# New SBUF addresses for matmul operands, and one VectorE instruction for four tiles, in a streaming encoder step

## The chip, the core and the metric

The kernel runs on one core of a Trainium2 chip. The metric is the device time of one execution, in microseconds (us). Engines are named as in the profile: PE is TensorE's matmul, PEld its weight load, DVE is VectorE, ACT ScalarE, POOL GpSimd, SP SyncE, which issues the DMAs.

## What is computed

One inference step of a one-layer encoder on 2048 prompt frames and 32 sample frames (T = 2080, D = 1024), all in float32:

```python
# norm -> one projection -> two attention groups -> one output projection
qa, ka, va, qb, kb, vb = split_proj(rmsnorm(h, g_attn), w_in)
oa = diff_attn(qa, ka, va)      # 4 heads: softmax(map 1) - lam * softmax(map 2), chunk-causal over all keys
ob = band_attn(qb, kb, vb)      # 8 heads: each 64-frame chunk sees itself and 8 chunks before
h = h + merge(oa, ob) @ w_out
# squared-ReLU MLP, gated input embedding, final norm
c = rmsnorm(h, g_mlp)
h = h + square(relu(c @ w_up)) @ w_down
h = h + sigmoid(h @ w_ple_gate) * (p @ w_ple_proj)
y = rmsnorm(h, g_final)
```

New keys and values are outputs too. The sample frames attend to a cache of 128 rows as well.

## The kernel before

Every product is made of three matmuls. An operand is split into a high part (rounded to the matmul type) and a low part (what is left), and `mm3` adds high x high, high x low and low x high into one PSUM bank; these are lines L220, L221 and L222 of the profile. The splitting is ACT's (high part, L182) and POOL's or DVE's (low part, L167, L177, L188). In a matmul row such as `vps<-wh,aH` the first name behind the arrow is the moving operand, whose columns stream through the array (256, 272 or 512 here), and the second is the stationary one (128 x 128).

The frames are cut into four blocks: 512, 512, 512 and 544 columns; the last is worked on as two halves of 272 columns. The stages, with the tiles that the change touches:

- Projection (`vwide`, `vtile`, `proj`). Values: `vps`, moving operand the value weights (`wh0`, `wl0` with 512 columns in the first stretch; `wh`, `wl` as two sets of [4, 256] afterwards, made by `wunit`), stationary the activations aH and aL. Queries and keys: `qps`, moving operand the activations.
- Long-range attention (`attn_a_pair`): scores `s` from the keys `ka` (moving), exponent, transposes `tpp` into `pH` and `pL`, and `o`, whose moving operand is `pH` or `pL` with 256 columns. Band attention (`attn_b_pair`) has scores `sb` and the sum `ob` from `pb`. Projections of other blocks are woven between the steps of attention; a list scheduler with its own timeline sets the order on every engine.
- Output projection `ops`, MLP (`ups`, `dps`) and gate (`gps`, `pps`). Blocks 0 and 1 use a plain MLP. Blocks 2 and 3 use `mlp7`, which makes seven quarter products in place of eight: `ups` from the ring `cs` (256 or 272 columns), then `dps` from `uh` and `ul`. These two, the parts of the output projection (`ou`), of the gate (`hu`) and of the input embedding (`pT`), and a few temporaries live in one ring of 20 tiles on the right side of SBUF, the pool `uh`, called up: the late ring. Each of its tiles has 544 columns (2176 bytes). Weights come as halves named `piece`.
- Final norm (`final`). For block 3, its last form (`end`) scales the tiles by the gain beforehand and multiplies at the end by the row factor y, half by half: tile 7 on DVE (L1405), tiles 5 and 6 on POOL (L167), tiles 4 and 3 to 0 on DVE (L1413), with a store after tile 4 and one after tile 0.

Pools take their addresses from two stacks, one from each end of a partition; a small tile opened first, such as `edge`, shifts all that comes after it.

Of the kernel before, what the change touches and what calls it, by code (L numbers as in the profile page):

```python
# [13 lines left out]
F32 = mybir.dt.float32  # L14
F32R = mybir.dt.float32r
# [5 lines left out]
P = 128  # L21
# [121 lines left out]


class Kern:
    def __init__(self, tc, a):
        self.tc = tc
        self.nc = tc.nc
        self.a = a
        self.nt = 3  # L150
        self.pieces = None

    def dma(self, dst, src):
# [455 lines left out]
    def attn_a_pair(self, g, j, ka, ba, pool, ps_s, ps_t, ps_o, late, first=None):  # L609
# [186 lines left out]
    def attn_b_pair(self, h, j, kt, v, kb, bb, q, t1, pool, ps_s, ps_t, ps_o, step, late):  # L796
# [9 lines left out]
        for qi, t in enumerate(tiles):  # L806
# [37 lines left out]
            def second(qi=qi, nr=nr, kts=kts, held=held, end=t is tiles[-1]):  # L844
                if qi == 0:
                    px.append(pool.tile([P, 6, 2, 256], F32R, tag="p", bufs=2, name="pb"))
                p = px[0]
                e = held[0]
# [65 lines left out]
    def oload(self, b, wk, up, out, r=None):  # L914
# [8 lines left out]
        elif up.whole:  # L923
            oact = [up.tile([P, 8, up.aw], F32R, tag="act", name="oact") for _ in range(2)]
            oact = [[t[:, k, :n] for k in range(8)] for t in oact]
        else:
            oact = [[up.tile([P, up.aw], F32R, tag="u", name="ou")[:, :n] for k in range(8)] for _ in range(2)]
        out[b] = oact
# [60 lines left out]
    def cparts(self, b, wk, cs, out, r):  # L989
# [34 lines left out]
    def cstage(self, b, up, out, r):  # L1024
# [6 lines left out]
        def parts(k, *which):  # L1031
            for x, raw in which:
                t = up.tile([P, up.aw], F32R, tag="u", name="cst")[:, :n]
                self.split(t[:, :m], t[:, m:], raw, "act", "dve")
                self.dma(out[x][:, :, k], t.rearrange("p (i c) -> p i c", i=2))

        late = ()
        for k in range(4):
            c = []
            for i in range(2):  # L1040
                tmp = up.tile([P, up.aw], F32, tag="u", name="ct")[:, :n]
                kk = k + 4 * i
# [127 lines left out]
    def mlp7(self, b, hh, box, ops, wk, up, mm, md):  # L1170
# [83 lines left out]
        for ch in range(DFF // (2 * P)):  # L1254
# [29 lines left out]
    def hparts(self, b, wk, up, out):  # L1284
        n, t0 = BN[b], 512 * b
        hH, hL = [[up.tile([P, BLK], F32R, tag="u", name="hu")[:, :n] for k in range(8)] for _ in range(2)]
        out.append((hH, hL))
# [7 lines left out]
    def ptile(self, b, up, wk):  # L1295
        n, t0 = BN[b], 512 * b
        pT = [[up.tile([P, up.aw], F32R, tag="u", name="pT") for _ in range(2)] for _ in range(2)]
        for k in range(2):
            raw = (
                up.tile([P, up.aw], F32, tag="u", name="praw") if wk is None  # L1300
                else wk.tile([P, BLK], F32, tag="tmp", bufs=self.nt, name="praw")
# [5 lines left out]
    def gate(self, b, h, up, act, md, wk=None, made=None, pT=None):  # L1307
# [13 lines left out]
        else:  # L1321
            hH, hL = [[up.tile([P, BLK], F32R, tag="u", name="hu")[:, :n] for k in range(8)] for _ in range(2)]
        if made is None:
            for k in range(8):
                self.split(hH[k], hL[k], h[:, k, :n], "act", "dve" if k % 2 else "pool")
        for dq in range(2):
            ph, pl = self.wunit(a["w_ple_proj"][dq], [2, 512])
            for d4 in range(4):
                d = 4 * dq + d4
                wh, wl = self.wunit(a["w_ple_gate"][d], [8, P])  # L1330
                for s0, sn in SUBS[b]:
# [5 lines left out]
                    sg = (  # L1337
                        up.tile([P, up.aw], F32, tag="u", name="sig") if wk is None
                        else wk.tile([P, BLK], F32, tag="tmp", bufs=self.nt, name="sig")
# [28 lines left out]
    def final(self, b, h, wk, mm):  # L1368
# [22 lines left out]
        for s0, sn in SUBS[b]:  # L1391
# [14 lines left out]
            for k in range(6, -1, -1):  # L1406
                hv = h[:, k, sub]
                if not end:
                    nc.vector.scalar_tensor_tensor(hv, hv, self.g_final[:, k : k + 1], y, op0=ALU.mult, op1=ALU.mult)  # L1409
                elif k in (5, 6):  # L1410
                    self.pool_tt(hv, hv, y, ALU.mult)
                else:
                    nc.vector.tensor_tensor(hv, hv, y, op=ALU.mult)  # L1413
# [296 lines left out]
```

## Time and profile before

| | |
|---|---|
| median of 3 runs | 3025.55 us (3023.77 to 3027.49) |
| profiled execution | 3025.88 us, its span 3023.8 us |
| PE busy | 2925.0 us, 97% of the span, 17217 matmuls |
| DVE, ACT, POOL busy | 60%, 58%, 62% |
| granted PE clock, mean | 0.990 |

The span runs from the first to the last instruction. A row of grouped instructions gives line, engine, operation, the tiles, the shape and the count; behind the bar the busy time and the mean duration of one; then the engine's idle time before them, with what ended it. Matmuls are pipelined: one starts long before the one ahead of it has ended, so the time that a stream takes is read from the starts. In a table by stretch of time, each engine has its busy time and, in brackets, its instructions; then come the granted PE clock, the share of DMA time and GB/s. A wait is given as total us, times, longest us.

### The profile page before, as it was taken

What the parts mean: (1) busy time and instruction counts of PE and PEld (TensorE: products, weight loads), DVE (VectorE), ACT (ScalarE), POOL (GpSimd) and SP (SyncE); (2) the same over time, 40 slices, a digit from 0 to 9 for tenths busy, and PEclk for the clock granted to TensorE, in tenths of its full rate; (3) what the DMA queues carried; (4) which work ended last, traced back from release to release, by engine and by line L of the source; (5) the groups of instructions that cost most, each with busy time, mean ns of one, the idle gap of its engine ahead of it and who ended that gap; (6) DMA issues with size and microseconds to landing.
All of it is one profiled execution on the core that took longest, in us unless ns stands there. A gap on an engine that the chain in (4) does not pass through costs nothing. (4 is left out here: it accounts for less than half of the span.)

```text
span 3023.8 us, 49919 instructions
## 1 busy us (share of the span) xinstructions
PE 2925.0 (97%) x17217; PEld 2576.6 (85%) x17217; DVE 1823.2 (60%) x4217; ACT 1746.1 (58%) x3226; POOL 1887.1 (62%) x2509
## 2 busy tenths in 40 slices
PE   8999999999989999999999999999999999999997
PEld 6798889999877888888888888778788887999997
DVE  5256554676565554667566566445677885677664
ACT  5365554777666665655665655554655455555455
POOL 2568775323465444666655655787688888787774
PEclk9999999999999999999999999999999999999999
DMA  9877867987887453655643543446423446323231
GB/s 311 283 235 237 242 205 220 272 238 223 251 251 219 136 152 105 188 150 168 207 143 124 149 141 111 157 157 209 162 91 134 142 142 239 129 91 119 98 103 54
DMA packets 295204, 528.45 MB, mean 175 GB/s; under 512 B 36316, under 2 KB 159232, under 8 KB 294952
## 3 DMA queue, kind: packets, MB, share of 16 engines
q1 hardware_dynamic: 294952, 525.27, 55.7%
q8 instruction: 136, 2.23, 0.3%
q14 instruction: 116, 0.95, 0.1%
HBM read 424.66 MB, written 104.45 MB: 175 GB/s over the span
## 5 line engine op out<-in xcount | busy, mean ns | idle before, releaser
L177 POOL TENSOR_TENSOR wl<-wr,wh 128x256 fp32r<-128x256 f32 x632 | 472.0, 780 | 246.2 <-ACT wh L182 218.3
L182 ACT ACTIVATE piece<-wr 128x512 fp32r<-128x512 f32 x406 | 245.4, 624 | 290.4 <-PE ups L221 131.2
L177 POOL TENSOR_TENSOR piece<-wr,piece 128x256 fp32r<-128x256 f32 x404 | 338.2, 862 | 93.5 <-ACT piece L182 87.0
L182 ACT ACTIVATE wh<-wr 128x1024 fp32r<-128x1024 f32 x228 | 240.0, 1055 | 200.2 <-PE ups L221 42.6
L167 POOL TENSOR_TENSOR wl<-wr,wh 128x256 fp32r<-128x256 f32 x280 | 216.6, 805 | 202.1 <-ACT wh L182 199.9
L220 PE MATMUL dps<-uh,piece 128*128 128x272 f32 (+1 forms) x768 | 246.7, 325 | 10.3 <-ACT piece L182 6.8
L167 POOL TENSOR_TENSOR piece<-wr,piece 128x256 fp32r<-128x256 f32 x280 | 237.2, 879 | 18.2 <-ACT piece L182 14.9
L222 PE MATMUL dps<-uh,piece 128*128 128x272 f32 (+1 forms) x768 | 247.1, 324 | 1.5 <-POOL piece L167 1.0
L221 PE MATMUL dps<-ul,piece 128*128 128x272 f32 (+1 forms) x768 | 247.0, 323 | 0.1
L221 PE MATMUL ups<-cs,piece 128*128 128x256 f32 (+1 forms) x864 | 244.8, 283 | 0.0
L220 PE MATMUL ups<-cs,piece 128*128 128x256 f32 (+1 forms) x864 | 244.8, 283 | 0.0
L222 PE MATMUL ups<-cs,piece 128*128 128x256 f32 (+1 forms) x864 | 244.7, 284 | 0.0
L220 PE MATMUL qps<-aH,wh 128*128 128x512 f32 (+1 forms) x640 | 227.4, 356 | 5.8 <-DVE ql L502 4.2
L221 PE MATMUL qps<-aL,wh 128*128 128x512 f32 (+1 forms) x640 | 227.2, 355 | 0.0
L222 PE MATMUL qps<-aH,wl 128*128 128x512 f32 (+1 forms) x640 | 226.7, 355 | 0.0
L665 ACT ACTIVATE e<-e,nm 128x128 f32<-128x128 f32 (+16 forms) x136 | 157.2, 1156 | 109.6 <-DVE nm L663 109.1
L1150 DVE TENSOR_TENSOR h<-h,dps 128x512 f32<-128x512 f32 x256 | 173.1, 681 | 69.0 <-PE dps L222 67.8
L1193 DVE TENSOR_TENSOR h<-h,dps 128x272 f32<-128x272 f32 (+1 forms) x384 | 188.8, 513 | 42.3 <-PE dps L222 41.7
L220 PE MATMUL dps<-uh,wh 128*128 128x512 f32 x512 | 204.7, 400 | 5.6 <-DVE h L1150 4.5
L220 PE MATMUL ups<-cH,wh 128*128 128x512 f32 x512 | 202.5, 396 | 0.0
L222 PE MATMUL ups<-cH,wl 128*128 128x512 f32 x512 | 202.3, 395 | 0.0
L221 PE MATMUL ups<-cL,wh 128*128 128x512 f32 x512 | 202.2, 395 | 0.0
(312 smaller groups left out, 9139.7 us busy)
## 6 DMA issues: line engine op xcount, KB each, us to landing
wr<-w_up SPq DMA_DIRECT2D x128, 512.0 KB, 3.5
wr<-w_down SPq DMA_DIRECT2D x128, 512.0 KB, 3.5
q<-qS SPq DMA_DIRECT2D x128, 256.0 KB, 5.2
v<-vSa SPq DMA_DIRECT2D x64, 512.0 KB, 4.6
wr<-w_qk SPq DMA_DIRECT2D x50, 512.0 KB, 5.0
ka<-kS SPq DMA_DIRECT2D x32, 512.0 KB, 7.4
wr<-w_out SPq DMA_DIRECT2D x32, 512.0 KB, 4.5
wr<-w_ple_gate SPq DMA_DIRECT2D x32, 512.0 KB, 4.1
```

Of the source, the lines that this page charges most:

```text
L167: nc.gpsimd.tensor_tensor(out[:, sl], a[:, sl], b[:, sl], op=op)
L177: nc.gpsimd.tensor_tensor(out[:, sl], a[:, sl], b[:, sl], op=op)
L182: nc.scalar.activation(hi, raw, AF.Copy)
L220: nc.tensor.matmul(ps, lh, rh, start=start and i == 0, stop=False)
L221: nc.tensor.matmul(ps, lh, rl, start=False, stop=False)
L222: nc.tensor.matmul(ps, ll, rh, start=False, stop=stop and i == n - 1)
L665: nc.scalar.activation(row, row, AF.Exp, bias=nmx, accum_out=z[:nr, m : m + 1])
L1150: nc.vector.tensor_tensor(hv, hv, ps, op=ALU.add)
L1193: nc.vector.tensor_tensor(hv, hv, ps, op=ALU.add)
```

## The change

Nothing that is computed changes but the grouping in the last norm. Tiles move:

- value weights `wh`, `wl` get a slot of 1152 columns, and the [4, 256] form starts 48 columns (192 bytes) into it;
- a filler of 48 columns ahead of `pH` and `pL` and one of 80 behind them; fillers of 96 and 32 around the band weights `pb`; one of 120 in the first pool; `edge` grows from 24 to 56 columns;
- the late ring (class `Even`) has tiles of 576 columns (2304 bytes), and a tile wider than 512 starts 32 columns (128 bytes) into its slot;
- `cs` keeps its place by an offset of 48 in place of 16.

In the built programs the start addresses, modulo 256 bytes, become:

| operand | columns | matmuls | before | after |
|---|---|---|---|---|
| moving: `wh`, `wl` of the values | 256 | 1248 | 0 | 192 |
| moving: `pH`, `pL` | 256 | 768 | 128 | 192 |
| moving: `wh0`, `wl0` | 512 | 192 | 96 | 0 |
| moving: `ka` | 128 to 512 | 656 | 0 and 128 | 0 |
| moving: late ring (`uh`, `ul`, `ou`, `hu`, `pT`) | 512 | 1440 | 0 and 128 | 0 |
| moving: `uh`, `ul` | 272 | 1536 | 0, 64, 128, 192 | 128, 192 |
| moving: `cs` | 256 | 1344 | 192 | 192 |
| moving: activations in `qps`, `pb` in `ob` | | | 0; 128 | the same |
| stationary: `piece` | | | three in four 0, else 128 | 0 |
| stationary: values in `o` | | | 128 | 0 |
| stationary: queries and values of the band | | | 0 | 128 |

In the last norm POOL takes tiles 4 and 5 instead of 5 and 6, DVE tile 6, and one DVE instruction tiles 0 to 3, with y broadcast over them.

```diff
+class Even:
+    def tile(self, shape, dt, tag, name):
+        w = shape[1]
+        t = self.pool.tile([P, 576], dt, tag=tag, name=name)
+        o = 32 if w > 512 else 0
+        return t[:, o : o + w]
...
-            hi = self.wp.tile([P] + shape, F32R, tag="wh", bufs=3, name="wh")
-            lo = self.wp.tile([P] + shape, F32R, tag="wl", bufs=3, name="wl")
+            o = 48 if shape == [4, 256] else 0
+            hi, lo = [
+                self.wp.tile([P, 1152], F32R, tag=x, bufs=3, name=x)[:, o : o + 1024].rearrange(
+                    "p (k c) -> p k c", c=shape[1]
+                )
+                for x in ("wh", "wl")
+            ]
...
+            fresh = pool is not self.spaced
+            if fresh:
+                self.spaced = pool
+                pool.tile([P, 48], F32, tag="gap0", bufs=1, name="gap")
             pH = pool.tile([P, 4, 256], F32R, tag="pH", bufs=2, name="pH")
             pL = pool.tile([P, 4, 256], F32R, tag="pL", bufs=2, name="pL")
+            if fresh:
+                pool.tile([P, 80], F32, tag="gap1", bufs=1, name="gap")
...
-            ops[x] = [t[:, 16 : 16 + 4 * m].rearrange("p (k c) -> p k c", c=m) for t in tiles]
+            ops[x] = [t[:, 48 : 48 + 4 * m].rearrange("p (k c) -> p k c", c=m) for t in tiles]
...
-                us.append([up.tile([P, up.aw], F32R, tag="u", name=x)[:, :n] for x in ("uh", "ul")])
+                us.append([up.tile([P, n], F32R, tag="u", name=x) for x in ("uh", "ul")])
...
-                elif k in (5, 6):
+                elif k in (4, 5):
                     self.pool_tt(hv, hv, y, ALU.mult)
-                else:
+                elif k == 6:
                     nc.vector.tensor_tensor(hv, hv, y, op=ALU.mult)
+                elif k == 0:
+                    hv = h[:, :4, sub]
+                    nc.vector.tensor_tensor(hv, hv, y.unsqueeze(1).broadcast_to((P, 4, sn)), op=ALU.mult)
...
-            opened(top, "edge", 1, side="right").tile([P, 24], F32, name="edge")
+            opened(top, "edge", 1, side="right").tile([P, 56], F32, name="edge")
...
+                pp.tile([P, 120], F32, tag="gap", bufs=1, name="gap")
...
-            up = Sized(opened(top, "uh", 20, side="right"), BLK)
+            up = Even(opened(top, "uh", 20, side="right"), BLK)
```

The scheduler writes another order with the new addresses, in the first sixth of the PE's instructions and at one place in the output projection of block 2; elsewhere the order is the same. On PE, before, the first long-range scores (`s`) stand among the projections `qps` of the same group of heads:

```order
L220 MATMUL qps<-aH,wh 128x512
L221 MATMUL qps<-aL,wh 128x512
L222 MATMUL qps<-aH,wl 128x512
L650 MATMUL s<-ka,q 128x128 x4
L220 MATMUL qps<-aH,wh 128x512
```

On PE, after, at the same scores (line numbers are those of the changed kernel):

```order
L240 MATMUL qps<-aL,wh 128x512
L241 MATMUL qps<-aH,wl 128x512
L669 MATMUL s<-ka,q 128x128 x4
L239 MATMUL vps<-wh,aH 128x256
L240 MATMUL vps<-wl,aH 128x256
L241 MATMUL vps<-wh,aL 128x256
```

Before, 264 of the 384 matmuls `qps` of the first group stand ahead of these scores and 120 behind them; after, all 384 stand ahead, and the value projections `vps` of the other group follow the scores.

On DVE, before, the end of the program, one half of block 3 in the last norm (`ry` is the row factor, `h` the tiles):

```order
L1402 TENSOR_TENSOR sqy<-sqy,ry 128x272
L1403 SCALAR_TENSOR_TENSOR ry<-sqy,ry 128x272
L1405 SCALAR_TENSOR_TENSOR h<-h,g_final_s,ry 128x272
L1413 TENSOR_TENSOR h<-h,ry 128x272 x5
L1401 SCALAR_TENSOR_TENSOR sqy<-sqy,ry 128x272
```

On DVE, after, at the same place:

```order
L1433 TENSOR_TENSOR sqy<-sqy,ry 128x272
L1434 SCALAR_TENSOR_TENSOR ry<-sqy,ry 128x272
L1436 SCALAR_TENSOR_TENSOR h<-h,g_final_s,ry 128x272
L1444 TENSOR_TENSOR h<-h,ry 128x272
L1447 TENSOR_TENSOR h<-h,ry 128x4x272
L1432 SCALAR_TENSOR_TENSOR sqy<-sqy,ry 128x272
```

Five multiplications of 272 columns have become one of 272 and one of four times 272, and the first step of the second half stands behind them as before.

More of the change, by code (lines that the diff above doesn't have):

```diff
@@ L142, in tile, with __init__ @@
         return self.pool.tile(*args, **kw)
+class Even:
+    whole = False
+    def __init__(self, pool, aw):
+        self.pool, self.aw = pool, aw
+    def tile(self, shape, dt, tag, name):
[3 more added lines that the diff above has]
+        return t[:, o : o + w]
 class Kern:
@@ L151, in __init__ @@
         self.pieces = None
+        self.spaced = None
     def dma(self, dst, src):
@@ L845, in second @@
                 if qi == 0:
+                    fresh = pool is not self.spaced
+                    if fresh:
+                        self.spaced = pool
+                        pool.tile([P, 96], F32, tag="gap0", bufs=1, name="gap")
                     px.append(pool.tile([P, 6, 2, 256], F32R, tag="p", bufs=2, name="pb"))
+                    if fresh:
+                        pool.tile([P, 32], F32, tag="gap1", bufs=1, name="gap")
                 p = px[0]
@@ L926, in oload @@
         else:
-            oact = [[up.tile([P, up.aw], F32R, tag="u", name="ou")[:, :n] for k in range(8)] for _ in range(2)]
+            oact = [[up.tile([P, n], F32R, tag="u", name="ou") for k in range(8)] for _ in range(2)]
         out[b] = oact
@@ L1032, in parts @@
             for x, raw in which:
-                t = up.tile([P, up.aw], F32R, tag="u", name="cst")[:, :n]
+                t = up.tile([P, n], F32R, tag="u", name="cst")
                 self.split(t[:, :m], t[:, m:], raw, "act", "dve")
@@ L1040, in cstage @@
             for i in range(2):
-                tmp = up.tile([P, up.aw], F32, tag="u", name="ct")[:, :n]
+                tmp = up.tile([P, n], F32, tag="u", name="ct")
                 kk = k + 4 * i
@@ L1285, in hparts @@
         n, t0 = BN[b], 512 * b
-        hH, hL = [[up.tile([P, BLK], F32R, tag="u", name="hu")[:, :n] for k in range(8)] for _ in range(2)]
+        hH, hL = [[up.tile([P, n], F32R, tag="u", name="hu") for k in range(8)] for _ in range(2)]
         out.append((hH, hL))
@@ L1296, in ptile @@
         n, t0 = BN[b], 512 * b
-        pT = [[up.tile([P, up.aw], F32R, tag="u", name="pT") for _ in range(2)] for _ in range(2)]
+        pT = [[up.tile([P, n], F32R, tag="u", name="pT") for _ in range(2)] for _ in range(2)]
         for k in range(2):
             raw = (
-                up.tile([P, up.aw], F32, tag="u", name="praw") if wk is None
+                up.tile([P, n], F32, tag="u", name="praw") if wk is None
                 else wk.tile([P, BLK], F32, tag="tmp", bufs=self.nt, name="praw")
@@ L1321, in gate @@
         else:
-            hH, hL = [[up.tile([P, BLK], F32R, tag="u", name="hu")[:, :n] for k in range(8)] for _ in range(2)]
+            hH, hL = [[up.tile([P, n], F32R, tag="u", name="hu") for k in range(8)] for _ in range(2)]
         if made is None:
@@ L1337, in gate @@
                     sg = (
-                        up.tile([P, up.aw], F32, tag="u", name="sig") if wk is None
+                        up.tile([P, sn], F32, tag="u", name="sig") if wk is None
                         else wk.tile([P, BLK], F32, tag="tmp", bufs=self.nt, name="sig")
```

## The prediction

> **What bounds the kernel now.** I read the page's head first, then a table of busy time by stage, then the PE's waits.
>
> ```profile
> span 3023.8 us, 49919 instructions
> PE 2925.0 (97%) x17217; PEld 2576.6 (85%) x17217; DVE 1823.2 (60%) x4217; ACT 1746.1 (58%) x3226; POOL 1887.1 (62%) x2509
> ```
>
> ```profile
> 0.00:500.00 500.00, 474.42 (x2708) 410.45 (x2709) 266.41 (x680) 267.26 (x527) 310.85 (x429) 0.99 0.79 247
> 1000.00:2000.00 1000.00, 993.80 (x5059) 837.15 (x5058) 588.77 (x1434) 599.93 (x986) 587.37 (x824) 1.00 0.48 148
> 2170.00:2560.00 390.00, 379.00 (x2290) 332.19 (x2289) 288.36 (x428) 206.61 (x393) 319.20 (x369) 1.00 0.44 153
> ```
>
> ```profile
> PE vps L220 <- ACT wh L182: 8.9, 1, 8.9
> PE s L650 <- DVE e L657: 3.6, 2, 2.1
> PE qps L220 <- DVE ql L502: 3.0, 1, 3.0
> ```
>
> The first column after each stretch is the PE's busy time: 474 of 500 us at the start, 994 of 1000 us in the middle. No other engine passes 62%. The three waits shown, among the PE's longer ones, sum to 15.5 us in 3024. So the kernel is a stream of matmuls, and it gets shorter when the spacing of matmuls gets shorter, wherever the next one is already released. Spacing is read from start times, since a matmul's duration overlaps the next one. Four stretches of the PE's timeline, each given by its first and last row:
>
> ```profile
> 365.73 0.28 PE L220 MATMUL vps<-wh,aH 128*128 128x256 f32 x1
> ...
> 367.89 0.28 PE L220 MATMUL vps<-wh,aH 128*128 128x256 f32 x1
> ```
>
> ```profile
> 1310.31 0.28 PE L723 MATMUL o<-pH,v 128*128 128x256 f32 x1
> ...
> 1311.75 0.28 PE L723 MATMUL o<-pH,v 128*128 128x256 f32 x1
> ```
>
> ```profile
> 2205.23 0.29 PE L220 MATMUL ups<-cs,piece 128*128 128x256 f32 x1
> ...
> 2206.61 0.28 PE L220 MATMUL ups<-cs,piece 128*128 128x256 f32 x1
> ```
>
> ```profile
> 84.65 0.39 PE L222 MATMUL qps<-aH,wl 128*128 128x512 f32 x1
> ...
> 88.05 0.39 PE L221 MATMUL qps<-aL,wh 128*128 128x512 f32 x1
> ```
>
> The value projection (vps) makes 18 steps in 2.16 us: 120.0 ns each. The weighted sum of attention (o) makes 12 steps in 1.44 us: 120.0 ns. The up products (ups) make 12 steps in 1.38 us: 115.0 ns. All three stream 256 columns. The 512-column projection takes 3.40 us for 15 steps, 226.7 ns, or 113.3 ns per 256 columns. So 120 ns is not the floor for 256 columns. What sets the three apart in the program is the moving operand's start: vps starts 0 bytes past a multiple of 256, o starts 128 past, ups starts 192 past. The change puts vps and o at 192.
>
> **The change part by part.** The groups kept apart by shape carry the counts (last number before the bar: how many; after it: busy us, mean ns of one):
>
> ```profile
> L220 PE MATMUL ups<-cs,piece 128*128 128x256 f32 x432 | 120.2, 278 | 0.0
> L221 PE MATMUL vps<-wl,aH 128*128 128x256 f32 x384 | 109.1, 286 | 0.0
> L724 PE MATMUL o<-pL,v 128*128 128x256 f32 x256 | 73.1, 285 | 0.0
> L222 PE MATMUL vps<-wh,aL 128*128 128x512 f32 x64 | 26.1, 408 | 0.0
> L220 PE MATMUL dps<-uh,piece 128*128 128x512 f32 x256 | 100.5, 398 | 9.0 <-ACT piece L182 6.8 <-DVE h L1193 1.6 <-ACT uh L182 0.6
> L221 PE MATMUL dps<-ul,piece 128*128 128x512 f32 x256 | 100.3, 393 | 0.1
> L221 PE MATMUL gps<-hL,wh 128*128 128x512 f32 x64 | 24.9, 391 | 0.4 <-POOL hL L167 0.4
> L221 PE MATMUL dps<-ul,piece 128*128 128x272 f32 x512 | 146.7, 288 | 0.0
> L650 PE MATMUL s<-ka,q 128*128 128x512 f32 x400 | 124.2, 399 | 0.3 <-DVE mx L659 0.3
> ```
>
> *Value weights, 256 columns.* Three lines of 384 full tiles, 1152 matmuls, and 96 more for the 32-row sample tile: 1248. The means, 286 against 278, differ by 8 ns; the starts by 5.0 ns. Bounds: 0 if the address is not the cause, -8 x 1248 = -10.0 us. The means of vps also hold a few stretches with pauses, and ups groups differ among themselves, so I take two thirds of the spacing difference, 3.3 ns: **-4.1 us**.
>
> *Long-range weights pH, pL.* Three lines of 256: 768 matmuls; 120.0 against 115.0 by the starts, 285 against 278 by the means. Bounds 0 and -5.4 us. Here the stage is nearly without idle time (994 of 1000 us), so I take 3.8 ns: **-2.9 us**.
>
> *First value projection, 512 columns, start 96 to 0.* 192 matmuls at 408 against 391 at start 0 (gps). Bounds 0 and -3.3 us; its mean also holds the first tens of us, where the PE waits for weights anyway. **-0.5 us**.
>
> *Late ring, 512 columns.* The ring u held tiles of 2176 bytes, so starts alternate between 0 and 128; now all are at 0. dps takes 398, 398 (its third line, taken like the first) and 393 against 391 for gps at 0, on 768 matmuls, and output projection, gate and input embedding add 672 of the same kind. If all 1440 went from about 396 to 391, that is -7.2 us; the lower bound is 0, since half of them stand at 0 already and the means hold waits for the weight pieces that address does not touch. I take 0.8 ns on all: **-1.2 us**. The weight pieces, a quarter of which started at 128, go to 0 with them; this is inside the same bounds.
>
> *Late ring, 272 columns.* 1536 matmuls, starts 0, 64, 128, 192 before; 128 and 192 now. The one mean, 288, mixes them. In the rows above a mean stands some 163 to 165 ns over the spacing (278 and 115.0, 285 and 120.0), so 288 is worth about 124 ns of spacing, or 117 per 256 columns, between 115 and 120. If the half at 0 and 64 carried the whole 5 ns, 768 x 5 = -3.8 us; the bound on the other side is the same, +3.8, should 64 be the good one. **-0.7 us**.
>
> *Key ring ka.* Score matmuls, about half at 128 before, all at 0 now; 400 of them are 512 wide. 399 against 391 on half of 400: -1.6 us at best, 0 at worst. **-0.4 us**. The band keeps its weights pb at 128 as before, while its queries and values (stationary) go from 0 to 128: by the same 8 ns at most on some 800 matmuls +6 us, but weights are loaded beside a running matmul (PEld 2577 us lies inside PE 2925 us), so I put 0.
>
> *The last norm.* The end of the timeline:
>
> ```profile
> 3011.50 1.92 POOL L167 TENSOR_TENSOR h<-h,ry 128x272 f32<-128x272 f32 x2 [17.91 <-DVE ry L1403]
> 3011.62 0.43 ACT L1400 ACTIVATE ry<-ry 128x272 f32<-128x272 f32 x1
> 3011.81 2.97 DVE L1413 TENSOR_TENSOR h<-h,ry 128x272 f32<-128x272 f32 x5
> 3014.70 0.43 DVE L1401 SCALAR_TENSOR_TENSOR sqy<-sqy,ry 128x272 f32<-128x272 f32 x1
> 3017.13 2.40 DVE L1413 TENSOR_TENSOR h<-h,ry 128x272 f32<-128x272 f32 x5
> L385 DVE TENSOR_TENSOR xt<-xt,g_attn_s x18: 424/1222/1752, 4.5 to 382.8; 128x1024 f32<-128x1024 f32 x15, 128x512 f32<-128x512 f32 x2, 128x256 f32<-128x256 f32 x1
> ```
>
> The second half's L1401 starts at 3014.70 though ACT delivered ry at 3012.05: it stands behind five multiplications of the first half, 2.97 us. After them come the second half's five, 2.40 us, then the last store. Both are on the path. The new form is one single multiplication (0.43 us) and one of 4x272 = 1088 elements. Its nearest row is L385, a multiplication of 1024 elements with a broadcast operand: median 1.22 us, so about 1.30, and up to 1.75 beside POOL. That is 1.73 to 2.2 us instead of 2.97 and 2.40: between -1.9 and -0.4 us for both; none if the long instruction and POOL's pair hold each other up. **-0.8 us**. POOL keeps two tiles, so its pair costs the same; the store of tiles 4 to 7 now ends on POOL, which is done before DVE.
>
> *Order.* The PE's order changes in the first sixth. All 384 projections qps of the first long-range group now stand ahead of the first scores, where 120 of them used to fill behind; value projections fill there now. SP's loads move with them. The sum of work is the same, and the waits are re-dealt: the PE is idle 500 - 474.4 = 25.6 us there. I put 0, with -6 to +12 us as bounds (a quarter of it gone; half as much again). Some of the vps gain lies in that stretch and is taken back by a wait that ends when DVE or ACT ends: **+1.6 us**.
>
> Sum: -4.1 - 2.9 - 0.5 - 1.2 - 0.7 - 0.4 - 0.8 + 1.6 = -9.0 us. The profiled execution took 3025.9 us with a span of 3023.8, 2.1 us around it, and stands 0.3 us above the median of 3025.55. So its span would come to 3014.8 and the median to **3016.5 us**.
>
> Two rules bear on the spacing. The Trainium skill, SBUF — State Buffer, Specifications (TRN2), gives 16-byte cachelines with full bandwidth on consecutive accesses to a line; every start here is a multiple of 32 bytes before and after, so by that rule alone the three streams would be alike and only the norm would count. The trace has 120.0 and 115.0 ns for the same column count, which that rule does not explain, but the three streams also differ in weights and stage, so it stays in the running as a rival. The Trainium skill, TensorE: Matmul & The Clock Gate, Back-to-back issue gap, gives N / 2.4 + 2.5 ns warm, an estimate of 109.2 ns for 256 columns; by it the 2016 moved matmuls could give up to 10.8 ns each, 22 us, and no 256-column row here comes that low.
>
> **The rivals.**
>
> *The address is not the cause.* Then 120 ns belongs to the stages of vps and o, whose weights, neighbours and DMA traffic differ (DMA share, the number before the last, 0.79 and 0.48 against 0.44 for ups), and comes along to any address. For it: nothing in the trace of before changes the address alone. Against: 0.48 and 0.44 hardly differ, and the 512-column qps at 226.7 ns runs in the stage with 0.79. Time: the norm alone, 3025.55 - 0.8 = 3024.7 us. Chance 0.20.
>
> *The new order starves the attention of the first stretch (slower).* The scores' chain (scores, DVE, exponent, DVE, transposes) runs while fillers run. With 120 qps of 0.227 us gone from behind the first scores, 27 us of cover are replaced by vps matmuls that need weights loaded and split just then (L177 and L167 on POOL). Existing waits there: s for DVE 3.6, qps for DVE 3.0. It decides when the idle time of the first 500 us rises from 25.6 to above 41 us, that is, when it eats the 9 us and 6 more. A long idle also lowers the clock afterwards:
>
> ```profile
> 2005.16 0.51 PE L220 MATMUL ops<-ou,piece 128*128 128x512 f32 x1 [2.56 <-ACT piece L182]
> 2007.10 0.63 PE L220 MATMUL ops<-ou,piece 128*128 128x512 f32 x1
> 2007.53 0.63 PE L221 MATMUL ops<-ou,piece 128*128 128x512 f32 x1
> ```
>
> After 2.56 us of waiting, starts are 0.43 us apart instead of 0.23. Five more such waits of 2.6 us, each with some ten slow matmuls (2 us), give +23 us against -9: about 3039 us. Chance 0.16.
>
> *Everything moved settles at the floor.* 2016 matmuls at 6.7 ns less (120.0 to 113.3), 13.5 us, the late ring 3, the norm 1.5: 3025.55 - 18 = 3007.5 us. Chance 0.12.
>
> **How the numbers follow.** The forecast has 0.52; 0.2% of the time, 6 us, is about what a measurement of this kernel can tell from no change. Faster by more: most of the forecast (0.50) and the last rival, 0.62. Within it: the address rival and the edge of the forecast, 0.22. Slower: 0.16. The range runs from the third rival, 3007, up past no change to 3030, where half as much idle again in the first stretch has eaten the gain; it leaves out the far end of the slower rival and a little below.
>
> **What would show it.** Right: starts of vps and o 115 ns apart at 256 columns, mean duration 278 to 280 in place of 285; two long DVE rows at the end, DVE done 1 us earlier after the last matmul; idle time of the first 500 us within some 6 us of 25.6. Wrong: vps and o still at 120 ns; the 272-column rows above 288; the first stretch with new waits of s, tpp or vps of over 2 us, or a lower clock there.

## The result, and the profile after

The changed kernel takes 3011.06 us (median of 5 runs, 3010.1 to 3015.49) against 3026.31 us for the kernel before (5 runs, 3023.77 to 3027.49). The ratio is 0.9958 with a 95% interval of 0.9946 to 0.9971: 12.7 us less, between 8.8 and 16.3 (the two medians lie 15.3 us apart). The forecast was 3016.5 us with 3007 to 3030 as its range, and faster as the likeliest sign. The profiled execution took 3015.49 us, the longest of the five, with a span of 3012.9 us.

Head of the page, changed kernel:

```profile
span 3012.9 us, 49893 instructions
PE 2910.3 (97%) x17217; PEld 2568.5 (85%) x17217; DVE 1827.4 (61%) x4211; ACT 1745.2 (58%) x3226; POOL 1883.8 (63%) x2509
```

The span is 10.9 us shorter. PE's busy time fell by 14.7 us with the same number of matmuls, so its idle time rose by 3.8 us. The same three stretches of time as in the prediction, changed kernel (PE's busy time is the first number after the comma):

```profile
0.00:500.00 500.00, 476.19 (x2768) 412.86 (x2769) 276.93 (x683) 267.83 (x530) 317.47 (x438) 0.99 0.80 251
1000.00:2000.00 1000.00, 991.50 (x5043) 834.09 (x5042) 589.25 (x1429) 601.48 (x988) 587.29 (x826) 1.00 0.49 147
2170.00:2560.00 390.00, 381.34 (x2281) 336.63 (x2280) 284.45 (x422) 207.71 (x395) 323.06 (x376) 1.00 0.45 154
```

The first 500 us hold 2768 matmuls where they held 2708, with 23.8 us idle in place of 25.6. The counts of the third stretch cannot be compared: the first up product of block 2 starts at 2165.9 us now, ahead of the window, and started at 2174.5 before, inside it. From that product to the last `dps` of block 2 the kernel took 349.6 us before and 348.7 now, hardly less.

PE's timeline, changed kernel, first and last row of a stretch: the value projection, the weighted sum, and the up products that the prediction showed:

```profile
344.99 0.28 PE L239 MATMUL vps<-wh,aH 128*128 128x256 f32 x1
...
347.03 0.28 PE L239 MATMUL vps<-wh,aH 128*128 128x256 f32 x1
```

```profile
1304.15 0.28 PE L748 MATMUL o<-pH,v 128*128 128x256 f32 x1
...
1305.57 0.28 PE L748 MATMUL o<-pH,v 128*128 128x256 f32 x1
```

```profile
2197.03 0.28 PE L239 MATMUL ups<-cs,piece 128*128 128x256 f32 x1
...
2198.45 0.28 PE L239 MATMUL ups<-cs,piece 128*128 128x256 f32 x1
```

vps: 18 steps in 2.04 us, 113.3 ns each, where 120.0 stood. o: 12 steps in 1.42 us, 118.3 in place of 120.0. ups: 12 steps in 1.42 us, 118.3 ns, where it had 115.0, although its start modulo 256 was kept. No part of the change was aimed at ups. (The rows round starts to 10 ns. By the trace's own nanoseconds the stretches of o and ups have 117.75 ns, so what reads as 118.3 here is the pace called 117.7 below.)

One stretch of the down products `dps` of block 2, the same six steps in the kernel before (starts at 128, 0, 128 and so on) and in the changed one (all at 0):

```profile
2200.60 0.40 PE L220 MATMUL dps<-uh,piece 128*128 128x512 f32 x1
...
2201.98 0.39 PE L220 MATMUL dps<-uh,piece 128*128 128x512 f32 x1
```

```profile
2192.44 0.39 PE L239 MATMUL dps<-uh,piece 128*128 128x512 f32 x1
...
2193.80 0.39 PE L239 MATMUL dps<-uh,piece 128*128 128x512 f32 x1
```

1.38 us and 1.36 us for six steps: 230 ns before, 226.7 ns now. Now the grouped rows of the changed kernel that answer to those of the prediction:

```profile
L240 PE MATMUL ups<-cs,piece 128*128 128x256 f32 x432 | 121.2, 281 | 0.0
L240 PE MATMUL vps<-wl,aH 128*128 128x256 f32 x384 | 107.9, 283 | 0.0
L749 PE MATMUL o<-pL,v 128*128 128x256 f32 x256 | 72.1, 282 | 0.0
L240 PE MATMUL dps<-ul,piece 128*128 128x512 f32 x256 | 100.3, 393 | 0.0
L240 PE MATMUL dps<-ul,piece 128*128 128x272 f32 x512 | 146.6, 288 | 0.0
```

The mean durations follow the 256-column streams (286 to 283, 285 to 282, 278 to 281). For the ring they say nothing: `dps<-ul` has 100.3 us and 393 ns in both kernels while its starts moved on average some 3 ns closer. A group's mean duration is not the pace of its stream.

DVE's end, changed kernel:

```profile
3001.15 1.00 DVE L1444 TENSOR_TENSOR h<-h,ry 128x272 f32<-128x272 f32 x1
3002.07 1.84 DVE L1447 TENSOR_TENSOR h<-h,ry 128x1088 f32<-128x1088 f32 x1
3003.83 0.43 DVE L1432 SCALAR_TENSOR_TENSOR sqy<-sqy,ry 128x272 f32<-128x272 f32 x1
...
3005.67 1.00 DVE L1444 TENSOR_TENSOR h<-h,ry 128x272 f32<-128x272 f32 x1
3006.59 1.84 DVE L1447 TENSOR_TENSOR h<-h,ry 128x1088 f32<-128x1088 f32 x1
```

The single multiplication takes 1.00 us beside POOL's pair, not 0.43, and the long one 1.84. The kernel before shows the same: the five multiplications of the second half, one row of 2.40 us in the prediction, begin with this one, and the other four, which start when POOL's pair is done, take 0.43 us each:

```profile
3017.13 0.99 DVE L1413 TENSOR_TENSOR h<-h,ry 128x272 f32<-128x272 f32 x1
```

SP's issue of the last two stores, of tiles 4 to 7 and of tiles 0 to 3, before and after:

```profile
3018.19 0.37 SPq L158 DMA_DIRECT2D y_t<-h  x1
3019.56 0.37 SPq L158 DMA_DIRECT2D y_t<-h  x1
```

```profile
3007.31 0.37 SPq L172 DMA_DIRECT2D y_t<-h  x1
3008.45 0.37 SPq L172 DMA_DIRECT2D y_t<-h  x1
```

The last matmul starts at 3010.10 us before and at 2999.45 after. Counted from it, the first of the two stores is issued at 8.09 us before and 7.86 after, the second at 9.46 and 9.01. In the trace the packets of both stores run without a gap, from 8.99 to 12.21 us before and from 8.76 to 11.98 after, 3.22 us each time. So the packets of the second store are held up by those of the first, and the end of the program follows the first store, 0.23 us earlier, and not the long multiplication.

### The profile page after: what moved, and what is told of

Its sections match the earlier page's. It is cut to its first block, busy times and chain, and to the rows that moved or that the text cites. A ratio compares the mean times of both kernels' runs of the same rounds, so it can differ in the third digit from the quotient of the medians.

```text
span 3012.9 us, 49893 instructions
## 1 busy us (share of the span) xinstructions
PE 2910.3 (97%) x17217; PEld 2568.5 (85%) x17217; DVE 1827.4 (61%) x4211; ACT 1745.2 (58%) x3226; POOL 1883.8 (63%) x2509
```

## The experiments

A ratio is to the kernel before, run beside it on the same chip. Two sums worked out from all starts of the PE go with it. *Stream* adds up what each start lies behind the one ahead of it beyond 113.3 ns per 256 columns, where that is under 25 ns: the pace of running streams. *Pauses* adds up the rest. Of the first, four kernels that differ little (changed, e5, e9, e10) have 40.7 to 41.5 us, so it repeats within about 1 us; of the second they have 219 to 224. Pauses also hold the slow steps in stretches where the granted clock stood at half of full speed: about 23 us of them before, 16 in the changed kernel and 19 to 25 in the others of the table. A difference of a few us in pauses, or in the span of one profile, is therefore no sign of the addresses.

| kernel | ratio (95%) | stream us | pauses us |
|---|---|---|---|
| before | | 52.2 | 220.0 |
| changed | 0.9958 (0.9946 to 0.9971) | 41.5 | 219.4 |
| e1_late: late ring alone | 0.9992 (0.9983 to 1.0001) | 49.2 | 218.0 |
| e8_order: new order alone | 0.9987 (0.9977 to 0.9997) | 51.8 | 214.9 |
| e3_v0: changed, value weights back at 0 | 0.9962 (0.9948 to 0.9977) | 45.1 | 219.3 |
| e9_t2: changed, one set of cs at 128 | 0.9963 (0.9951 to 0.9975) | 41.5 | 223.4 |
| e10_once: changed, 12 matmuls more | 0.9961 (0.9946 to 0.9976) | 40.7 | 221.3 |
| e11_ring192: changed, ring at 192 | 0.9975 (0.9964 to 0.9986) | 45.3 | 223.3 |
| e12_ul: changed, ul at 128 | 0.9979 (0.9968 to 0.9990) | 41.6 | 223.8 |

Five more kernels (e2, e4, e5, e6, e7) ran once each, for their traces: 3017.1, 3015.2, 3018.8, 3022.0 and 3018.2 us.

**Value weights back at 0 (e3_v0).**

```diff
-            o = 48 if shape == [4, 256] else 0
+            o = 0
```

> The changed kernel with the 256-column value weights back at 0 modulo 256 in the same slots; order and all other addresses are those of the changed kernel. Theory A: vps at 256 columns goes back from about 115.5 to about 119 to 120 ns apart, 1248 x 3.3 to 4 ns = +4 to +5 us against the changed kernel, about 3015.5 us. Theory B (the gain of vps came from the new order of the first stretch): no change, vps stays at 115.5 ns, about 3011 us.

The same 18 steps of the value projection as above, e3_v0:

```profile
345.30 0.28 PE L239 MATMUL vps<-wh,aH 128*128 128x256 f32 x1
...
347.45 0.28 PE L239 MATMUL vps<-wh,aH 128*128 128x256 f32 x1
```

2.15 us, 119.4 ns, against 113.3: one number in the program changed, the order did not. Over the kernel the stream sum rises from 41.5 to 45.1 us, 3.6 us for 1248 matmuls. For these matmuls the address sets the pace. The timed ratios (0.9962 and 0.9958) cannot tell 3.6 us apart, the starts can.

**The late ring alone (e1_late).**

```diff
+            opened(top, "edge2", 1, side="right").tile([P, 32], F32, name="edge2")
-            up = Sized(opened(top, "uh", 20, side="right"), BLK)
+            up = Even(opened(top, "uh", 20, side="right"), BLK)
...
-            ops[x] = [t[:, 16 : 16 + 4 * m].rearrange("p (k c) -> p k c", c=m) for t in tiles]
+            ops[x] = [t[:, 48 : 48 + 4 * m].rearrange("p (k c) -> p k c", c=m) for t in tiles]
```

> The kernel before with the late ring of the change alone (slots of 576 columns, everything 512 wide at 0 modulo 256, 272 wide at 128 and 192), in the order of before on every engine. Theory A, the moving operand's start sets the pace: the 512-column matmuls of dps, gps, ops and pps that stood at 128 start about 227 instead of 231 to 232 ns apart, 1440 x about 4 ns = -5.6 us, so about 3020 us against 3025.5. Theory B, the pace belongs to the stage or to the order of instructions: their starts stay at 230 to 231 ns and the time within 1 us of before. The prediction's own term for this part was -1.2 (512 columns) and -0.7 us (272 columns). A second question is read from the same trace: the up products ups, 256 columns, whose ring cs keeps its start of 192 but moves down by 2560 bytes with the ring; in the changed kernel they slowed from 115 to 117.6 ns. If the ring's part of the change does it, they run at 117.6 here too.

The 512-column matmuls of the ring start 227 to 228 ns apart where they had 231 on average, and their part of the stream sum falls by 5.4 us. (In the built program the weight pieces, their stationary operands, go to 0 along with the ring here, a quarter of them from 128. e11_ring192 below keeps them at 0 and moves the ring alone, and the pace changes again.) The second question has its answer too. Group of the up products in e1_late:

```profile
L234 PE MATMUL ups<-cs,piece 128*128 128x256 f32 x432 | 121.7, 282 | 0.0
```

282 ns where before has 278: their spacing goes from 115.3 to 117.6 ns on the mean, and their part of the stream sum rises by 2.8 us. So the ring's part gives back nearly half of its own gain; the stream sum falls by 3.0 us net, and the ratio puts it at -2.4 us (-5.1 to +0.3).

**Why ups lost: its address or what runs ahead of it (e5_cs1536).**

```diff
+            opened(top, "edge2", 1, side="right").tile([P, 384], F32, name="edge2")
             cs = Sized(opened(top, "cs", 14, side="right"), None)
```

> The changed kernel with a filler of 1536 bytes ahead of the ring cs, so that cs lies 4096 bytes below its place in the kernel before (2560 in the changed kernel) and keeps its start of 192 modulo 256. Theory A, bits of the address above 256 decide between the two paces of ups (113.3 and 117.7 ns): back to the mixture of before, mean 115.3 ns. Theory C, the pace is taken over from the stream ahead (dps and pps from the late ring, now all at 0) and the address of cs beyond its start does not matter: 117.6 ns as in the changed kernel.

Groups of twelve ran at 117.7 ns, 92 of 94, as in the changed kernel (90 of 94). Moving cs to 4096 bytes below its first place did not bring the fast pace back; a dependence on bits at or above 4096 is not excluded by this run, but e10_once below has both paces at one address.

**A sweep of starts (e2_cs, e6_cs16, e7_cs2, e4_v).** The seven sets of cs get starts of their own:

```diff
-            tiles = [cs.tile([P, 4 * 272], F32R, tag="cs", name="cs") for _ in range(2)]
-            ops[x] = [t[:, 48 : 48 + 4 * m].rearrange("p (k c) -> p k c", c=m) for t in tiles]
+            tiles = [cs.tile([P, 4 * 272], F32R, tag="cs", name=nm[x]) for _ in range(2)]
+            ops[x] = [t[:, at[x] : at[x] + 4 * m].rearrange("p (k c) -> p k c", c=m) for t in tiles]
```

> The changed kernel, its seven sets of operands of the up products (block 2, 256 columns) at seven different starts modulo 256: 0, 64, 128, 192, 32, 224, 96 (named csa to csg in the order of the products); nothing else differs. Theory A, the start alone sets the pace: the set at 0 runs at 120 ns, as the values did at 0, the one at 128 at 120 as o did, the one at 192 between 113.3 and 117.7, the others in between, the same in every chunk. Theory B, the pace belongs to the stage: all seven at 117.6. Theory C, there are paces that a stream falls into and keeps until something disturbs it: sets in the same gap between dps stretches run alike, whatever their start.

> The changed kernel, its seven sets of operands of the up products (256 columns) at starts that are odd multiples of 16 modulo 256: 16, 208, 160, 176, 80, 240, 48 (csa to csg in the order of the products). The set with starts a multiple of 32 gave 119.4 at 0, 116.9 at 32, 118.1 at 64, 119.1 at 96, 118.6 at 128, 118.3 at 224 and a fall to 113.3 within a group at 192. Theory A (a start has its own repeating pattern): each set again one pattern, the same in each chunk; one of them, 176 or 208 beside 192, may hold 113.3 throughout. If none does, 192 is the best start and about 4 ns of ups cannot be had by the start alone. Rival: below 32 bytes the start does not matter and each set runs like its neighbour.

Set csa, start 0, in e2_cs, nine steps:

```profile
2170.53 0.28 PE L239 MATMUL ups<-csa,lead 128*128 128x256 f32 x1
...
2171.61 0.28 PE L239 MATMUL ups<-csb,lead 128*128 128x256 f32 x1
```

1.08 us for nine, 120.0 ns: the pace that vps had at 0. Mean spacings, without steps that lie 25 ns or more over 113.3:

| start modulo 256 | 0 | 16 | 32 | 48 | 64 | 80 | 96 | 128 | 160 | 176 | 192 | 208 | 224 | 240 |
|---|---|---|---|---|---|---|---|---|---|---|---|---|---|---|
| ns | 119.4 | 118.2 | 117.0 | 118.4 | 118.1 | 118.8 | 120.5 | 118.5 | 117.5 | 118.7 | 117.2 | 118.6 | 118.4 | 117.2 |

Every start has its own repeating sequence of steps (at 64: 118, 117, 119, 117, 118, 118 and again), much the same in nearly every chunk. The mean at 96 is higher than the 119.1 that the expectation quotes: nearly every product of that set has a step of 132 or 133 ns, which belongs to its sequence and not to a wait. Only 192 showed runs of 113.3: in some of its groups the steps go 117, 117, 123, 118 and then stay at 113 and 114, in others they stay at 117 and 118. A start 16 bytes off (176, 208) does not have it. A set also has its fixed place in the chunk, but the two runs give each place two starts, and the sequence goes with the start.

> The changed kernel with the high and the low part of each set of the up products at different starts modulo 256: (192,0), (192,64), (192,128), (0,192), (128,192), (0,128), (64,192) for csa to csg. Theory A, each matmul is slowed by its own start: the mean lies between those of the two starts weighted two to one (119.4 and 117.7 for 0 and 192: 118.3 for csa, 118.8 for csd). Theory C, what counts is the step from one matmul's end to the next one's start: a pair can be faster than both (113.3) or slower than both (over 120).

With high and low part at different starts the means were 117.9, 117.8, 119.0, 118.1, 119.7, 117.3, 117.2 ns. They are not the weighted means of the single starts: (0,128) came out at 117.3, where both alone have 118.5 and more. What the matmul ahead did counts as well.

> The changed kernel with the 256-column value weights at eight starts in turn, unit by unit: 0, 32, 64, ... 224 modulo 256 (named wha to whh, wla to wlh). Theory A: a pace for each start, 119 to 120 ns at 0 and at 128, 113 to 116 at 192, and the others between or like one of these. Theory B: the units differ by their stage only, and no start stands out.

For the value weights, cycled through eight starts unit by unit, few groups of twelve are free of pauses (2 to 5 for each start). The means of all running steps (81 to 160 for each start) are 119.1 at 0, 116.1 at 192, and 117.1 to 119.0 at the others: 192 lowest again, but this run alone would prove little.

**Two paces at one start (e10_once, e9_t2).** e10_once issues, once in the whole kernel, twelve matmuls whose moving operand starts at 128; the product behind them overwrites what they wrote. e9_t2 puts one of the seven sets at 128 for good.

```diff
+            if b == 2 and self.kick and x == "t1":
+                self.kick = False
+                for i in range(12):
+                    y = ops["b11"][i % 2].rearrange("p k c -> p (k c)")
+                    nc.tensor.matmul(ps, w[0][:, 0], y[:, 48 : 48 + m], start=True, stop=True)
```

> The changed kernel with twelve extra matmuls of 256 columns, once, ahead of the fourth product of block 2's first chunk, whose moving operand starts at 128; their result is overwritten by the product. They cost 12 x 0.12 = 1.4 us. Theory C: the following products at 192 go over to 113.3 ns and stay there beyond the stretches of dps between, until something disturbs them; if they all do, -1300 x 4.4 ns = -5.7 us, net -4.3. Theory A: every later product stays at 117.7 ns, net +1.4 us. Between them: the fast pace lasts for some chunks and is lost again.

Up products in e10_once: the row in front of the twelve, the twelve (L1236), then a stretch 7 us later, then one 28 us later, behind dps:

```profile
2170.98 0.28 PE L242 MATMUL ups<-cs,lead 128*128 128x256 f32 x1
2171.10 1.60 PE L1236 MATMUL ups<-cs,lead 128*128 128x256 f32 x12
2172.54 0.28 PE L240 MATMUL ups<-cs,lead 128*128 128x256 f32 x1
...
2178.11 0.28 PE L241 MATMUL ups<-cs,piece 128*128 128x256 f32 x1
...
2179.47 0.28 PE L241 MATMUL ups<-cs,piece 128*128 128x256 f32 x1
...
2199.12 0.28 PE L240 MATMUL ups<-cs,piece 128*128 128x256 f32 x1
...
2200.54 0.28 PE L240 MATMUL ups<-cs,piece 128*128 128x256 f32 x1
```

Between 2178.11 and 2179.47 lie 12 steps, 113.3 ns each; in the changed kernel the same instructions had 117.7. From 2199.12 on, 12 steps take 1.42 us, 118.3 ns, again. In between stands dps, all at 0. So a stream at 192 has two paces, keeps the one that it is in for some 80 matmuls at least, and the stretch of dps at 0 sets it back here. In the changed kernel 49 of 53 entries from such a stretch ran at 117.6 or 117.8 (an entry is a run of twelve or more ups matmuls directly behind dps). In the kernel before, entries from dps with both starts in it fell on either pace, some six in ten on 113.3. That is how evening out the ring cost the products behind it. The net in time is nothing (0.9961).

> The changed kernel with one of the seven sets of the up products (t2, the third product of a chunk) at 128 in place of 192, in block 2. In the sweep of starts the product behind that set fell from 117.7 to 113.3 ns after some five matmuls. Theory C (a stream at 192 has two paces and keeps the one it is in): the products behind t2 run at 113.3 to 115, t2 itself at 118.5; up to 1152 x 4 ns = -4.6 us and 192 x 0.9 = +0.2 us against the changed kernel, about 3007 us. Theory A (the start alone): t2 a little slower, the other six unchanged at 117.7; about 3011.5 us.

The same, repeated, and with no matmul added: only the start of t2 differs, so the twelve extra matmuls as such are not needed. The six products between the first t2 and the next ran at 113.3 to 114.6; most later ones fell back to 117.7 after dps; the set at 128 ran at 119.2. No gain (0.9963).

**The ring at 192, and one in six of dps at 128 (e11_ring192, e12_ul).**

```diff
-        o = 32 if w > 512 else 0
+        o = 32 if w > 512 else 48
```

> The changed kernel with the 512-column tiles of the late ring at 192 in place of 0 modulo 256 (the start that the up products have too); 272-column tiles and all else as in the changed kernel. Theory A (192 is a good start for any width): dps, gps, pps stay at 227 ns, and ups may take over 113.3; 3006 to 3011 us. Theory C with a pace of its own for 512 columns at 192: dps between 227 and 232, up to 1440 x 4 = +6 us, and ups mixed between 113.3 and 117.7 after it, -3 us; 3009 to 3014 us.

The stretch of dps shown above, in e11_ring192, and the group of ups:

```profile
2198.88 0.39 PE L239 MATMUL dps<-uh,piece 128*128 128x512 f32 x1
...
2200.27 0.39 PE L239 MATMUL dps<-uh,piece 128*128 128x512 f32 x1
```

```profile
L239 PE MATMUL ups<-cs,piece 128*128 128x256 f32 x432 | 120.0, 278 | 0.0
```

1.39 us for six steps, 231.7 ns against 226.7 at 0 (over the whole ring 232.6 against 227.4): for 512 columns 192 is a bad start, for 256 columns it is the best that was tried. And ups is back at 278: from dps at 192 it goes over to 113.3 in two of three cases. Against the changed kernel the ring loses 7.8 us and ups gains 3.6; the stream sum rises from 41.5 to 45.3 us.

> The changed kernel with one tile of the late ring in four (the low part ul of the second half, the last but one matmul's operand in a product dps of block 2) at 128 in place of 0. In the trace of before, stretches of dps with both starts handed ups over to 113.3 ns in two of three cases; those all at 0 in the changed kernel hand it over to 117.7. Theory C: ups at 256 columns becomes a mixture, about 115 ns, 1344 x 2.5 = -3.4 us, against 128 to 256 matmuls of dps at 2 to 4 ns more, +0.7 us: net about -2.7 us, 3008 us where the changed kernel has 3011. Theory A (the start alone): ups stays at 117.7, and the kernel loses 0.7 us.

This is `odd=f == 1 and x == "ul"` passed to the ring's tile, with an offset of 32 for it. The moved matmuls, 128 of the 768 of dps, ran 234.0 ns to the next start in place of 227.4, their neighbours at 0 stayed at 227.5 to 227.8, and ups stayed at 117.7 in 85 of 94 groups. The guess that any other start within dps brings the fast pace back is wrong; what exactly decides the entry stays open.

**The new order alone (e8_order).** The value slots grow and a filler of 128 columns stands in the first pool; the scheduler then writes the changed kernel's order while every start modulo 256 stays as before.

```diff
+                pp.tile([P, 128], F32, tag="gap", bufs=1, name="gap")
```

> The kernel before with the new order alone: the value weights' slots grow to 1152 columns and a filler of 128 columns stands in the first pool, which makes the scheduler write the order of the changed kernel on every engine (but for the last norm), while every matmul operand keeps its start modulo 256 of before. The prediction put +1.6 us on the order, with -6 to +12 as bounds; the rival in which the scores starve gives +14 us or more. Milestones of the traces say what to expect: the first band score starts at 515.1 us in before, 514.0 with the late ring alone, 510.5 with the new order and the value weights at 0, 507.6 in the changed kernel. If the order is worth what these say, about -3 to -4 us by that point, and 3021 to 3023 us in all; if the 3 us came from the 192 first value projections at 0, about 0.

Band scores, first and last start, in before, e8_order and the changed kernel:

```profile
L831 PE MATMUL sb<-kbt,q x448: 223/309/477, 515.1 to 1166.6; 128*128 128x320 f32 x128, 128*128 128x128 f32 x6, 128*128 128x512 f32 x6, 128*128 128x256 f32 x5
```

```profile
L836 PE MATMUL sb<-kbt,q x448: 222/309/478, 509.5 to 1167.0; 128*128 128x320 f32 x128, 128*128 128x128 f32 x6, 128*128 128x512 f32 x6, 128*128 128x256 f32 x5
```

```profile
L856 PE MATMUL sb<-kbt,q x448: 221/309/636, 507.5 to 1160.9; 128*128 128x320 f32 x128, 128*128 128x128 f32 x6, 128*128 128x512 f32 x6, 128*128 128x256 f32 x5
```

With the order alone the band starts 5.6 us earlier, and ends at the same time: the lead is given back within it, in part in its waits (the output projection waits 12.6 us for ACT and DVE there, where before waits 10.1 for ACT, DVE and one load). The timed ratio is -3.9 us (-7.0 to -0.9). Where it comes from stays open. In the profiles e8_order is ahead of before by 1.0 us at the first gate matmul (1945.9 against 1946.9 us) and by 4.1 us at the first up product of block 2 (2170.4 against 2174.5); the order differs once more in between. But kernels that are one program up to the first gate matmul reached it anywhere from 1939.9 to 1948.4 us, so single profiles cannot place a gain of this size.

## Why the prediction was right, and where its terms were off

- **What bounds the kernel**: right. The kernel got shorter by the pace of running matmuls: stream sum -10.7 us, pauses -0.6 (a difference that chance alone can make).
- **Value weights, -4.1 us**: e3_v0 gives -3.6 by the stream sum, and vps alone has -4.1 from before to after. Right in cause and size. The pace is 113.3 or 117.7 rather than one 115, and the mean duration 280 to 283 rather than 278 to 280.
- **pH, pL, -2.9 us**: on the mean 119.5 to 116.8 ns, 768 x 2.7 = -2.1 us; 26 of 32 groups run at the slower pace of 192. That their own start did it is not shown: they were not run alone, and the values, their stationary operand, moved from 128 to 0 with them.
- **First value projection, -0.5 us, and keys, -0.4 us**: by the stream sums -0.9 (232.5 to 228.4 ns a step) and -0.3. Not run alone either, nor was the band.
- **Late ring, 512 columns, -1.2 us**: the term that was mis-sized. -5.4 us came in e1_late and -5.1 in the changed kernel, near the bound of -7.2. The step that failed was to price it by mean durations (398, 393, 391), which mix in waits and hardly moved (395 to 399 and 393 for dps after), when the starts of the same rows gave 231 ns against 226.7. Half of them stood at 0 already, and the prediction counted on those as good: in the kernel before, dps at 0 ran at 230.7 ns and at 128 at 231.7. Why those at 0 were slow as well is not shown; in e12_ul matmuls at 0 beside one at 128 kept their 227.5 to 227.8.
- **cs "keeps its place"**: no term stood for it, and it cost +2.8 us. The prediction took the start modulo 256 as the whole cause. A stream's pace also depends on the one ahead of it. The quoted stretch of 115.0 begins with steps of 124 and 117 ns and then runs at 113.3, while other groups of ups stood at 117.7; the table of groups hid that there are two paces.
- **Late ring, 272 columns, -0.7 us**: 125.4 to 124.9 ns on 1536, -0.8. Its 288 did not show it either: it is 288 in both kernels.
- **Last norm, -0.8 us, bounds -1.9 to -0.4**: counted from the last matmul, DVE was done 0.45 us earlier (8.98 against 9.43), SP's last issue 0.46 (9.37 against 9.83), and the span's end only 0.21 (13.48 against 13.69), outside the bounds. It repeats: the eleven kernels with the new norm end 13.46 to 13.49 us behind the last matmul, the three with the old one at 13.69 or 13.70. Two steps failed. The single multiplication was priced at 0.43 us from a row without POOL's pair beside it, when the first of the five took 0.99; it took 1.00, and the long one 1.84 against 1.30 to 1.75. And the second half's multiplications of tiles 0 to 3 were put on the path, when the last store was held up by the packets of the store ahead of it. The lower bound does not follow from its rows: 2.2 us in place of 2.97 and 2.40 is -1.0, and -0.4 had no row.
- **Order, +1.6 us**: the sign was wrong; e8_order has -3.9 (-7.0 to -0.9), within the bounds of -6 to +12. The cause is not known.
- **Rivals.** *The address is not the cause* falls with e3_v0 for vps and with e11_ring192 for the ring, each against the changed kernel at one fixed order. *The new order starves the attention*: its first stretch went faster; the given-back lead in the band is the nearest thing to it, and stays below its point of decision. *Everything settles at the floor*: true of vps in part and of the ring, not of o and ups.

The sum by what was measured: stream -10.7, norm -0.2, the order 0 to -4, together -11 to -15 us, inside the interval of -8.8 to -16.3. That the forecast of -9.0 came near is in part luck: the ring gave about 4 us more than its term and the order some 2 to 6 us more, while ups cost 2.8 us that had no term and pH, pL and the norm fell short by 1.4. By the 16-byte cachelines of the Trainium skill, SBUF — State Buffer, Specifications (TRN2), alone all these starts would be alike, since each is a multiple of 16; the sweep has 117.0 to 120.5 ns, and the measurement decides. The formula that the Trainium skill, TensorE: Matmul & The Clock Gate, Back-to-back issue gap, gives for an isolated matmul makes an estimate of 109.2 ns for 256 columns; the lowest pace that held here was 113.3.

No experiment beat the changed kernel: e9_t2 and e10_once, meant to, came out at 0.9963 and 0.9961.

## What to carry to other kernels

Read the pace of a matmul stream from its starts, group by group, and not from mean durations: at 512 columns the means hardly moved while the pace moved by 3 to 4 ns. Where two streams with the same column count differ by a few per cent, look at where the moving operand starts modulo 256 bytes, and try each width by itself; after such a move, read again the streams that run behind the moved one. A few us of a 3000 us kernel show in the sums of starts long before they show in its times. And before pricing the end of a kernel by its last instructions, look at which store's packets the last store waits behind.

## What the runs showed of the hardware

- For 256 columns a start at 0 gave 119.4 to 120 ns, at 192 113.3 or 117.7; for 512 columns a start at 0 gave 226.7 to 227.4, at 192 231.7 to 232.6 and at 128 mixed with 0 about 231. No start that was tried at both widths was best for both.
- One and the same instruction stream at one address has two stable paces, 113.3 and 117.7 ns. Twelve matmuls at another start put it from one to the other (e10_once), and so did one product of the stream itself at 128 (e9_t2).
- A DVE multiplication of 272 columns took 0.99 or 1.00 us beside POOL's pair, in both kernels, and 0.43 us behind it (in the kernel before); the one of 1088 columns took 1.84 us.
- Two stores of 544 KB, issued 1.4 or 1.1 us apart, moved as one train of packets of 3.22 us; issuing the second 0.45 us earlier ended it 0.21 us earlier, as the first one was issued 0.23 us earlier (all counted from the last matmul).
